# A block-triangular solve regrouped from two head pairs to four, and its rows emitted as a stream of their own

## Chip, cores and metric

One core of one Trainium2 chip runs the program in one launch. The metric is the device time of one execution in microseconds. Engines are named as the profile names them: PE (matmul), PEld (its weight loads), DVE (vector), ACT (scalar), POOL (GpSimd), SP (which here only issues DMAs); "ACTq" and "SPq" are DMA issues standing in an engine's instruction stream.

## What is computed

The network has a first block of two layers (retention, HGRN2, gated FFN) and a second block of two layers (sliding-window attention beside an RWKV7 recurrence, a conv FFN, a gated embedding). The sequence has 512 tokens, the model width is 1024. The change lies in the second block's mixer, in the recurrence, which has 16 heads of width 64:

```python
def step(state, inp):
    r_t, w_t, k_t, v_t, a_t, b_t = inp
    sa = jnp.einsum('bhvk,bhk->bhv', state, a_t)
    state = (state * w_t[:, :, None, :] + sa[..., None] * b_t[:, :, None, :]
             + v_t[..., None] * k_t[:, :, None, :])
    return state, jnp.einsum('bhvk,bhk->bhv', state, r_t)
```

The kernel does this in chunks of 64 tokens. A chunk needs the inverse of a unit lower triangular 64x64 matrix for each head; the kernel inverts its two 32x32 diagonal blocks by forward substitution on DVE and joins them by matmuls.

## The kernel before

Heads go in eight pairs, 0 to 7 (two heads of 64 on 128 partitions). For each of the second block's two layers `mixer2` does this:

- `rw_low` makes what all pairs share. Then the **attention stage**: the stream K (`keys`, which runs `rw_a` for a pair: projection, decays, and the triangular products into the tile `x2`, L1158) and the stream A (`attention`). `rw_a` of pairs 0 and 1 runs first alone, the rest beside attention.
- `rw_solve`, called by `keys` after each two pairs, sends the diagonal blocks through DRAM (`ls`) into `lu`, one block on a partition, so that 31 rows of the substitution work on all blocks at once. Each row is two DVE instructions, L1185 (`tm` = a column of `lu` times a row of `tt`) and L1186 (`tt` += `tm`), each needing the one before it. Two pairs have 2 pairs x 2 heads x 8 chunks x 2 blocks = 64 blocks; they stand twice on the 128 partitions, and each half of the partitions makes 16 of the 32 columns. The result goes to DRAM (`ts`, L1189). There are four such solves in a layer and eight in all.
- The **recurrence stage**: the stream `preps` (`rw_prep` of a pair: projections of r and v, loads of `wx`, `bk`, `x2` and of the solved blocks into `tb` at L1220, products) and the stream `seqs` (`rw_seq`: eight dependent steps, each a matmul L1317, a copy `sv` on DVE L1319 that the next step needs, and a copy on ACT L1320). A pair's prep waits for its solve and for the sequence two pairs back.

Projections are products of fp32 split into a high and a low part (L303, L304, L305); their weights are split by ACT (L287) and by POOL in the attention stage or DVE in the recurrence stage (L288). `interleave` merges the streams by a planned clock: a generator yields how long PE is busy and how long the stream then rests. `rw_solve` yields nothing, so in the plan a solve takes no time; `solved[b]` holds its planned end, 55 us after the call. The framework then moves instructions within each engine's stream by a model of its own, and each engine runs its stream in order. The tiles of the attention stage give their memory to those of the recurrence stage, so that `rdg` and `tb` are cleared (L1466, POOL) only when the last pair's `x2` has been read by its DMAs (L1174).

## Time and profile before

| what | value |
|---|---|
| time, median of 3 runs | 4030.81 us (4030.28 to 4038.12) |
| profiled execution, its own time | 4036.65 us |
| its span, first to last instruction | 4034.8 us |
| PE, DVE, ACT, POOL busy | 93%, 66%, 44%, 14% |
| mean granted clock of PE | 0.97 |

The span is what the profiler saw between the first and the last instruction of that execution; its own time is what was measured around it. A busy PE is not a PE at its peak, since matmuls overlap and their ends are modelled; the weight loads (PEld) follow the amount of matmul work more closely. In the first layer of the second block the attention stage runs from about 1495 to 1797 us and the recurrence from 1798 us to about 2110 us; the second layer repeats this 1300 us later.

### The profile page before, as it was taken

What the parts mean: (1) busy time and instruction counts of PE and PEld (TensorE: products, weight loads), DVE (VectorE), ACT (ScalarE), POOL (GpSimd) and SP (SyncE); (2) the same over time, 40 slices, a digit from 0 to 9 for tenths busy, and PEclk for the clock granted to TensorE, in tenths of its full rate; (3) what the DMA queues carried; (4) which work ended last, traced back from release to release, by engine and by line L of the source; (5) the groups of instructions that cost most, each with busy time, mean ns of one, the idle gap of its engine ahead of it and who ended that gap; (6) DMA issues with size and microseconds to landing.
All of it is one profiled execution on the core that took longest, in us unless ns stands there. A gap on an engine that the chain in (4) does not pass through costs nothing.

```text
span 4034.8 us, 56574 instructions
## 1 busy us (share of the span) xinstructions
PE 3762.3 (93%) x19888; PEld 3117.2 (77%) x19888; DVE 2667.9 (66%) x5595; ACT 1774.9 (44%) x3727; POOL 576.6 (14%) x515
## 2 busy tenths in 40 slices
PE   7998999999999988889999999998888989999998
PEld 6877888888888876657778888896665777888887
DVE  7888444555644567887664676687788775476667
ACT  4433333544433352435553554455344555354444
POOL 0201000110100033222110200014331220020001
PEclk9999999999999998989999999999888999999999
DMA  8466333312333343343227433344334323743334
GB/s 287 153 204 189 97 94 95 94 48 63 100 95 96 91 147 105 97 128 109 91 65 255 124 107 92 99 153 152 96 98 130 110 81 101 234 126 97 94 96 137
DMA packets 316573, 487.34 MB, mean 121 GB/s; under 512 B 79744, under 2 KB 127744, under 8 KB 316160
## 3 DMA queue, kind: packets, MB, share of 16 engines
q1 hardware_dynamic: 240256, 422.82, 34.0%
q10 hardware_dynamic: 76032, 60.90, 4.7%
q8 instruction: 157, 2.57, 0.3%
q14 instruction: 128, 1.05, 0.1%
HBM read 422.72 MB, written 60.88 MB: 120 GB/s over the span
## 4 chain that ended last, share of the span: by engine, by line
PE 55%; DVE 13%; ACT 3%; issue 3%; POOL 1%; DMA 1%; ACTq 0%; SPq 0%; POOLq 0%; DVEq 0%
PE ps L303 15%; PE ps L304 15%; PE ps L305 15%; DVE tm L1185 2%; PE ps L1317 1%; DVE tt L1186 1%; PE ps L1300 1%; PE ps L1157 1%; DVE ro L946 1%; DVE wl L288 1%; PE ps L983 1%; ACT wh L287 1%; PE ps L1023 1%; PE ps L1280 1%; PE ps L1285 1%
## 5 line engine op out<-in xcount | busy, mean ns | idle before, releaser
L303 PE MATMUL ps<-hi,wh 128*128 128x512 f32 (+1 forms) x4384 | 1635.3, 374 | 41.5 <-DVE ro L946 18.1
L305 PE MATMUL ps<-hi,wl 128*128 128x512 f32 (+1 forms) x4384 | 1622.1, 371 | 9.7 <-DVE wl L288 5.2
L304 PE MATMUL ps<-lo,wh 128*128 128x512 f32 (+1 forms) x4384 | 1622.7, 371 | 7.8 <-DVE lo L449 4.6
L287 ACT ACTIVATE wh<-raw 128x512 fp32r<-128x512 f32 (+1 forms) x1158 | 710.1, 620 | 1281.8 <-PE ps L304 1065.7
L288 DVE TENSOR_TENSOR wl<-raw,wh 128x512 fp32r<-128x512 f32 (+1 forms) x1005 | 690.8, 693 | 515.9 <-ACT wh L287 487.1
L303 PEld LDWEIGHTS ps<-hi,wh 128*128 128x128 f32 x4384 | 840.6, 192 | 181.3 <-issue 19.6
L305 PEld LDWEIGHTS ps<-hi,wl 128*128 128x128 f32 x4384 | 841.4, 192 | 143.7 <-DVE wl L288 7.8
L304 PEld LDWEIGHTS ps<-lo,wh 128*128 128x128 f32 x4384 | 842.5, 192 | 138.4 <-DVE lo L449 4.9
L288 POOL TENSOR_TENSOR wl<-raw,wh 128x512 fp32r<-128x512 f32 (+1 forms) x153 | 200.1, 1318 | 1193.2 <-ACT wh L287 1165.2
L1381 POOL TENSOR_TENSOR x<-x,ys 128x256 f32<-128x256 f32 x48 | 43.6, 909 | 862.9 <-DVE ys L1380 793.0
L482 DVE SCALAR_TENSOR_TENSOR ad<-ad,cact 128x1024 f32<-128x1024 f32 x96 | 116.7, 1220 | 29.2 <-DMA ad<-in_ada 29.1
L175 DVE TENSOR_TENSOR acc<-acc,sq 128x256 f32<-128x256 f32 (+1 forms) x175 | 96.1, 552 | 25.2 <-ACT sq L174 23.1
L1157 PE MATMUL ps<-bk,adg 128*128 128x192 f32 x256 | 67.2, 384 | 46.5 <-DVE bk L1147 20.5
L1319 DVE COPY sv<-ps 64x64 f32<-64x64 f32 x224 | 49.5, 221 | 90.4 <-PE ps L1317 87.6
L1185 DVE TENSOR_TENSOR tm<-lu,tt 128x126 f32<-128x126 f32 (+22 forms) x248 | 100.1, 404 | 9.0 <-DMA lu<-ls 4.0
L1580 DVE TENSOR_TENSOR u<-ps,r 128x512 f32<-128x512 f32 x88 | 60.5, 690 | 67.7 <-PE ps L305 67.0
L1317 PEld LDWEIGHTS ps<-sv,add 128*128 128x128 f32 (+1 forms) x512 | 77.9, 189 | 31.9 <-issue 8.8
L1292 POOL TENSOR_SCALAR add<-rdg 64x512 f32<-64x512 f32 x32 | 51.5, 1609 | 351.3 <-DVE add L1301 226.6
L1157 PEld LDWEIGHTS ps<-bk,adg 128*128 128x128 f32 x256 | 47.3, 216 | 64.8 <-issue 34.2
L1317 PE MATMUL ps<-sv,add 128*128 128x64 f32 (+1 forms) x512 | 91.1, 272 | 3.7 <-DVE sv L1319 2.3
L1320 ACT ACTIVATE y<-ps 64x64 f32<-64x64 f32 x256 | 54.7, 216 | 88.7 <-DVE sv L1319 49.5
L1186 DVE TENSOR_TENSOR tt<-tt,tm 128x126 f32<-128x126 f32 (+22 forms) x248 | 80.7, 325 | 3.7
(356 smaller groups left out, 5168.7 us busy)
## 6 DMA issues: line engine op xcount, KB each, us to landing
raw<-in_q_win SPq DMA_DIRECT2D x224, 256.0 KB, 2.9
ad<-in_ada SPq DMA_DIRECT2D x96, 512.0 KB, 4.4
raw<-in_q_w_up SPq DMA_DIRECT2D x184, 256.0 KB, 2.7
raw<-in_win SPq DMA_DIRECT2D x98, 256.0 KB, 3.1
raw<-in_w_val SPq DMA_DIRECT2D x92, 256.0 KB, 2.6
raw<-in_w_gate SPq DMA_DIRECT2D x92, 256.0 KB, 2.8
raw<-in_q_w_down SPq DMA_DIRECT2D x74, 256.0 KB, 2.6
raw<-in_w_down SPq DMA_DIRECT2D x64, 256.0 KB, 2.6
```

The source lines that it names most:

```text
L175: nc.vector.tensor_tensor(out=self.acc[:, cs], in0=self.acc[:, cs], in1=q, op=ADD)
L287: nc.scalar.activation(h, raw, AF.Copy)
L288: self.lo_eng.tensor_tensor(out=l, in0=raw, in1=h.bitcast(F32), op=SUB)
L303: nc.tensor.matmul(o, h, ah, start=k == first, stop=False)
L304: nc.tensor.matmul(o, h, al, start=False, stop=False)
L305: nc.tensor.matmul(o, l, ah, start=False, stop=k == last)
L482: nc.vector.scalar_tensor_tensor(out=raw, in0=raw, scalar=1.0, in1=self.cact, op0=MUL, op1=MUL, accum_out=m)
L1157: nc.tensor.matmul(o, ad[:, c], bk[:, c], start=True, stop=True)
L1185: nc.vector.tensor_tensor(out=t, in0=lc, in1=tt[:, 0:c, j:j + 1].to_broadcast([P, c, n]), op=MUL)
L1186: nc.vector.tensor_tensor(out=tt[:, 0:c, j + 1:32], in0=tt[:, 0:c, j + 1:32], in1=t, op=ADD)
L1317: nc.tensor.matmul(o, add[h][rows, c], c3(sv[h])[rows, c], start=True, stop=True)
L1580: nc.vector.tensor_tensor(out=u, in0=pj(ff), in1=r2, op=MUL)
```

## The change

One solve now takes four pairs, so 128 blocks, one on each partition, and every partition makes all 32 columns. Row j works on j + 1 columns instead of j // 2 + 1. There are two solves in a layer (`V` streams): the first for pairs 0 to 3 starts in the attention stage once pair 3's `x2` is there, the second for pairs 4 to 7 starts with the recurrence. Each row is emitted by itself and the stream then rests 3.5 us of planned time in the attention stage and 3.0 us in the recurrence. The blocks of each pair are sent to `ls` right after its `rw_a`, by the new `rw_lower`. The starting values `ttinit` become identity matrices; `lu`, `tt` and `tm` have one buffer each. `lu` is filled by one DMA and `ts` written by one, instead of two each.

```diff
--- before.py
+++ after.py
@@ -86,10 +86,7 @@
     hs[64:, 1] = 1.0
     c["hsel"] = hs
     c["blk1"] = np.kron(np.eye(2), np.ones((64, 64))).astype(np.float32)
-    tti = np.zeros((P, 16, 32), np.float32)
-    for cc in range(16):
-        tti[np.arange(P), cc, 2 * cc + np.arange(P) // 64] = 1.0
-    c["ttinit"] = tti
+    c["ttinit"] = np.tile(np.eye(32, dtype=np.float32), (P, 1, 1))
     c["rope2c"] = np.stack([invf[np.arange(P) % 32], np.where(q % 2 == 0, -1.0, 1.0)], axis=1).astype(np.float32)
     masks.append(mm == tt)
     c["lvmask"] = np.concatenate(masks, axis=1).astype(np.float32)
@@ -1162,33 +1159,34 @@
             nc.scalar.dma_start(st[n], src)
         yield 2.6, 1.0
 
-    def rw_solve(self, sts):
-
-
-        nc = self.nc
-        ls = self.dram("ls", (32, 2, 32, 32), 4)
-        for q, st in enumerate(sts):
-            for h in range(2):
-                for b in range(2):
-                    r, u = 64 * h + 32 * b, 16 * q + 8 * h
-                    nc.scalar.dma_start(ls[u:u + 8, b].rearrange("c t s -> t c s"), st["lm"][r:r + 32, :, 0, 32 * b:32 * b + 32])
+    def rw_lower(self, ls, i, x2):
+
+        for h in range(2):
+            for b in range(2):
+                r, u = 64 * h + 32 * b, 16 * i + 8 * h
+                self.nc.scalar.dma_start(ls[u:u + 8, b].rearrange("c t s -> t c s"), x2[r:r + 32, :, 0, 32 * b:32 * b + 32])
+
+    def rw_solve(self, sts, ls, gap):
+
+
+        nc = self.nc
         lu = self.rw.tile([P, 32, 32], F32, name=self.name("lu"), tag="lu", bufs=1)
-        tt = self.rw.tile([P, 16, 32], F32, name=self.name("tt"), tag="tt", bufs=2)
-        tm = self.rw.tile([P, 136], F32, name=self.name("tm"), tag="tm", bufs=2)
-        for m in range(2):
-            nc.sync.dma_start(lu[64 * m:64 * m + 64], ls.rearrange("u b t s -> (u b) t s"))
+        tt = self.rw.tile([P, 32, 32], F32, name=self.name("tt"), tag="tt", bufs=1)
+        tm = self.rw.tile([P, 256], F32, name=self.name("tm"), tag="tm", bufs=1)
+        nc.sync.dma_start(lu, ls.rearrange("u b t s -> (u b) t s"))
         nc.sync.dma_start(tt, self.I["ttinit"])
+        yield 0.0, 3.0
         for j in range(31):
-            n, c = 31 - j, j // 2 + 1
+            n, c = 31 - j, j + 1
             t = tm[:, 0:n * c].rearrange("p (c i) -> p c i", c=c)
             lc = lu[:, j + 1:32, j:j + 1].rearrange("p i o -> p o i").to_broadcast([P, c, n])
             nc.vector.tensor_tensor(out=t, in0=lc, in1=tt[:, 0:c, j:j + 1].to_broadcast([P, c, n]), op=MUL)
             nc.vector.tensor_tensor(out=tt[:, 0:c, j + 1:32], in0=tt[:, 0:c, j + 1:32], in1=t, op=ADD)
-        ts = self.dram("ts", (64, 16, 2, 32), 4)
-        for m in range(2):
-            nc.scalar.dma_start(ts[:, :, m], tt[64 * m:64 * m + 64])
+            yield 0.0, gap
+        ts = self.dram("ts", (128, 32, 32), 4)
+        nc.scalar.dma_start(ts, tt)
         for q, st in enumerate(sts):
-            st["ts"] = ts.rearrange("(u b) a m i -> u b (a m) i", b=2)[16 * q:16 * q + 16]
+            st["ts"] = ts.rearrange("(u b) a i -> u b a i", b=2)[16 * q:16 * q + 16]
 
     def mu_cols(self, l, j):
         i = self.idx[f"mu{l}"] + j
@@ -1433,14 +1431,21 @@
                         yield 5.2, 0.0
 
         st = [dict() for _ in range(8)]
-        solved = {-1: 0.0}
-
-        def keys(bs):
-            for b in bs:
-                for i in (2 * b, 2 * b + 1):
-                    yield from self.rw_a(l, i, H, st[i])
-                self.rw_solve(st[2 * b:2 * b + 2])
-                solved[b] = max(self.now + 4.0, solved[b - 1]) + 55.0
+        solved = {}
+        ls = [self.dram("ls", (64, 2, 32, 32), 4) for _ in range(2)]
+
+        def keys(pairs):
+            for i in pairs:
+                yield from self.rw_a(l, i, H, st[i])
+                self.rw_lower(ls[i // 4], i % 4, st[i]["lm"])
+                st[i]["lower"] = True
+
+        def solve(b, gap):
+            while "lower" not in st[4 * b + 3]:
+                yield 0.0, 0.5
+            yield 0.0, 2.0
+            yield from self.rw_solve(st[4 * b:4 * b + 4], ls[b], gap)
+            solved[b] = self.now + 3.0
 
         self.S = "G"
         for j in self.HEAD2[3:]:
@@ -1455,8 +1460,8 @@
             nc.gpsimd.memset(self.adg, 0.0)
             for t in self.bk:
                 nc.vector.tensor_copy(t[:, :, 2], self.id2.rearrange("p (o d) -> p o d", o=1).to_broadcast([P, 8, 64]))
-            self.interleave([("K", keys((0,)))])
-            self.interleave([("K", keys((1, 2, 3))), ("A", self.attention(l, H, od, pre[9]))])
+            self.interleave([("K", keys(range(2)))])
+            self.interleave([("V", solve(0, 3.5)), ("K", keys(range(2, 8))), ("A", self.attention(l, H, od, pre[9]))])
         with ExitStack() as es:
             self.rb = es.enter_context(self.tc.tile_pool(name="rb", bufs=1))
             self.rdg = [self.rb.tile([P, 8, P], F32, name=f"rdg{j}") for j in range(2)]
@@ -1468,7 +1473,7 @@
 
             def preps():
                 for i in range(8):
-                    while solved[i // 2] > self.now or i >= 2 and "seq" not in st[i - 2]:
+                    while solved.get(i // 4, 1e9) > self.now or i >= 2 and "seq" not in st[i - 2]:
                         yield 0.0, 0.5
                     yield from self.rw_prep(l, i, H, st[i])
 
@@ -1488,7 +1493,7 @@
                     nc.scalar.dma_start(md[m], g)
 
             self.lo_eng = nc.vector
-            self.interleave([("A", seqs()), ("K", preps())])
+            self.interleave([("V", solve(1, 3.0)), ("A", seqs()), ("K", preps())])
             self.S = "G"
             for _ in gates():
                 pass
```

In the rows of after, line numbers are two or three lower than those of the same code before: the solve's two lines are L1183 and L1184, the copy `sv` is L1317.

On DVE, in layer one, where the first solve of before begins (`lo` is the low half of small weights, `vt` an evacuation for attention, `t`, `ic`, `bk` belong to `rw_a` of pair 2). Before:

```order
L1065 TENSOR_SCALAR lw_13707<-lw_13707 128x512
L278 TENSOR_TENSOR lo_14150<-lora_14146,hi_14149 64x128
L1185 TENSOR_TENSOR tm_13397<-lu_13395,tt_13396 128x31
L1186 TENSOR_TENSOR tt_13396<-tt_13396,tm_13397 128x31
L1185 TENSOR_TENSOR tm_13397<-lu_13395,tt_13396 128x30
L1186 TENSOR_TENSOR tt_13396<-tt_13396,tm_13397 128x30
L1185 TENSOR_TENSOR tm_13397<-lu_13395,tt_13396 128x58
L1186 TENSOR_TENSOR tt_13396<-tt_13396,tm_13397 128x2x29
L1185 TENSOR_TENSOR tm_13397<-lu_13395,tt_13396 128x56
L1186 TENSOR_TENSOR tt_13396<-tt_13396,tm_13397 128x2x28
```

The same place after:

```order
L275 TENSOR_TENSOR lo_14084<-lora_14080,hi_14083 64x128
L965 COPY vt_13464<-ps_13614 128x512
L1138 TENSOR_SCALAR t_13876<-ic_13630,om_13058,om_13056 128x512
L1140 SCALAR_TENSOR_TENSOR ic_13630<-ic_13630,kk_13770 128x512
L1144 TENSOR_TENSOR bk_13141<-zs_13433,wi_13768 128x8x64
L1143 SCALAR_TENSOR_TENSOR bk_13141<-ic_13630,wi_13768 128x8x64
L940 TENSOR_TENSOR ro_13677<-ps_13640,cos_13454 128x512
```

The 62 solve instructions that began here are gone from this place, and `rw_a`'s and attention's own instructions (`ro` is attention's rotary step) follow each other. The first solve of after begins amid `rw_a` of pair 4, at about the place where the second solve of before stood; 231 places of the DVE stream lie between its first and its last instruction, with those of the other two streams between its rows.

On DVE, in the sequence of pair 0 (`sv` are the copies that the next step waits for). Before:

```order
L1319 COPY sv_15886<-ps_16161 64x64
L288 TENSOR_TENSOR wl_16332<-raw_16330,wh_16331 128x512
L1248 TENSOR_TENSOR zs_16047<-ps_16153,zs_16087 128x512
L1319 COPY sv_15887<-ps_16161 64x64
L1319 COPY sv_15886<-ps_16195 64x64
L288 TENSOR_TENSOR wl_16354<-raw_16352,wh_16353 128x512
L1319 COPY sv_15886<-ps_16247 64x64
L1319 COPY sv_15887<-ps_16195 64x64
L1319 COPY sv_15887<-ps_16247 64x64
```

The same place after:

```order
L1184 TENSOR_TENSOR tt_15569<-tt_15569,tm_15570 128x12x20
L1317 COPY sv_15677<-ps_15963 64x64
L1317 COPY sv_15676<-ps_15997 64x64
L1183 TENSOR_TENSOR tm_15570<-lu_15568,tt_15569 128x247
L1184 TENSOR_TENSOR tt_15569<-tt_15569,tm_15570 128x13x19
L1317 COPY sv_15676<-ps_16051 64x64
L1183 TENSOR_TENSOR tm_15570<-lu_15568,tt_15569 128x252
L1184 TENSOR_TENSOR tt_15569<-tt_15569,tm_15570 128x14x18
L1183 TENSOR_TENSOR tm_15570<-lu_15568,tt_15569 128x255
L1184 TENSOR_TENSOR tt_15569<-tt_15569,tm_15570 128x15x17
L1317 COPY sv_15677<-ps_15997 64x64
L1183 TENSOR_TENSOR tm_15570<-lu_15568,tt_15569 128x256
```

Rows of the second solve now stand between the copies; before, the last solve was over at this point. In the stream of after, the last row of this solve stands behind the `rdg` instructions of pair 3 and ahead of those of pair 4, whose prep is the first to need its result.

On ACT, at the end of the attention stage (`zs` evacuates pair 0's r projection for the recurrence, `wh` splits weights, the DMAs send pair 7's and pair 6's tiles). Before:

```order
L1162 DMA x_15690<-x_15665 128x1536
L1174 DMA ls_15692<-x_15382 32x8x32 x2
L1174 DMA ls_15692<-x_15665 32x8x32 x4
L1058 ACTIVATE zs_15822<-ps_15785,om_13054 128x512
L287 ACTIVATE wh_15827<-raw_15826 128x512
L287 ACTIVATE wh_15845<-raw_15844 128x512
L1424 ACTIVATE gt_18441<-ps_18442 128x512
```

After:

```order
L1159 DMA bk_15523<-bk_13142 1024x1x128
L1055 ACTIVATE zs_15610<-ps_15573,om_13054 128x512
L284 ACTIVATE wh_15810<-raw_15809 128x512
L284 ACTIVATE wh_15828<-raw_15827 128x512
L1055 ACTIVATE zs_15650<-ps_15613,om_13054 128x512
L284 ACTIVATE wh_18336<-raw_18335 128x512
L1159 DMA x_15525<-x_15496 128x1536
L1167 DMA ls_13076<-x_15496 32x8x32 x4
L284 ACTIVATE wh_15850<-raw_15849 128x512
```

The evacuations of pair 0 and the splits of pair 1's weights now stand ahead of the DMAs that wait for the last `x2`. On SP the loads of those weights likewise moved ahead of the load of `lu`.

## Rows read from the trace of the kernel before

**Rows 1.** The page: busy us, share of the span, instructions of each engine.

```profile
PE 3762.3 (93%) x19888; PEld 3117.2 (77%) x19888; DVE 2667.9 (66%) x5595; ACT 1774.9 (44%) x3727; POOL 576.6 (14%) x515
```

**Rows 2.** Stretches of both attention stages: length, busy of PE, PEld, DVE, ACT, POOL; PEclk, DMA, GB/s.

```profile
1560.00:1600.00 40.00, 27.41 (x101) 20.81 (x100) 36.68 (x86) 6.54 (x11) 14.89 (x13) 0.75 0.24 72
1600.00:1660.00 60.00, 55.42 (x274) 39.52 (x273) 49.18 (x123) 26.90 (x89) 20.24 (x17) 0.94 0.30 90
1680.00:1800.00 120.00, 101.99 (x463) 68.74 (x462) 101.62 (x304) 50.40 (x149) 23.54 (x20) 0.86 0.34 101
...
2860.00:2900.00 40.00, 27.40 (x101) 20.64 (x101) 33.99 (x82) 6.81 (x18) 14.24 (x12) 0.74 0.23 61
```

**Rows 3.** Chain that ended last, 1550:1605, 1670:1725, 1745:1800, 1800:1845, shares by line.

```profile
by line: DVE tm L1185 17.0%; issue 11.7%; PE ps L303 9.7%; PE ps L305 9.3%; DVE tt L1186 9.3%; DVE ro L946 8.8%; PE ps L304 8.6%; DMA lu<-ls 7.7%; DVE bk L1146 3.0%; POOL ro L947 2.4%; DVE ro L943 2.3%; POOL wl L288 2.3%; PE ps L983 1.5%; A
by line: issue 24.0%; DVE tm L1185 11.5%; DVE ro L946 10.1%; DVE tt L1186 8.8%; PE ps L1023 6.3%; PE ps L1157 5.6%; POOL adg L1150 5.3%; PE ps L1012 5.2%; PE ps L983 4.8%; PE ps L1121 3.8%; DVE x L1158 3.1%; PE ps L1133 2.9%; DVE lw L1065 2
by line: DVE tm L1185 12.0%; DVE tt L1186 11.9%; DMA lu<-ls 8.0%; PE ps L1157 7.2%; PE ps L1023 6.4%; DVE sc L988 5.0%; DVE x L1158 4.5%; DVE am L989 4.3%; PE ps L983 4.3%; issue 4.2%; ACTq L1174 4.2%; DVE sc L1001 3.8%; PE ps L1012 3.5%; D
by line: DVE tm L1185 19.8%; DVE tt L1186 16.4%; DVE rdg L1217 10.9%; DMA lu<-ls 9.8%; issue 8.9%; DVE zs L1228 7.1%; DVE wl L288 4.5%; DVE add L1301 3.4%; PE ps L304 2.8%; PE ps L303 2.8%; PE ps L305 2.8%; ACT rbb L1265 2.5%; DVE add L1243
```

**Rows 4.** The solve's two lines, 1545:1800 and then 1800:2100: busy us, mean ns.

```profile
L1185 DVE TENSOR_TENSOR tm<-lu,tt 128x126 f32<-128x126 f32 (+22 forms) x93 | 40.1, 431 | 2.9 <-DMA lu<-ls 2.0
L1186 DVE TENSOR_TENSOR tt<-tt,tm 128x126 f32<-128x126 f32 (+22 forms) x93 | 30.5, 328 | 1.1
...
L1185 DVE TENSOR_TENSOR tm<-lu,tt 128x126 f32<-128x126 f32 (+22 forms) x31 | 10.4, 335 | 2.3 <-DMA lu<-ls 1.6
L1186 DVE TENSOR_TENSOR tt<-tt,tm 128x126 f32<-128x126 f32 (+22 forms) x31 | 9.4, 302 | 0.7
```

**Rows 5.** Timeline of single solve instructions and one POOL instruction: start, us, what.

```profile
1556.16 0.21 DVE L1185 TENSOR_TENSOR tm<-lu,tt 128x31 f32<-128x31 f32 x1 [1.98 <-DMA lu<-ls]
1556.40 0.19 DVE L1186 TENSOR_TENSOR tt<-tt,tm 128x31 f32<-128x31 f32 x1
...
1557.47 1.28 POOL L288 TENSOR_TENSOR wl<-raw,wh 128x512 fp32r<-128x512 f32 x1 [3.77 <-ACT wh L287]
1557.64 1.18 DVE L1185 TENSOR_TENSOR tm<-lu,tt 128x56 f32<-128x56 f32 x1
...
1571.91 0.30 DVE L1186 TENSOR_TENSOR tt<-tt,tm 128x133 f32<-128x133 f32 x1
...
1581.49 0.39 DVE L1185 TENSOR_TENSOR tm<-lu,tt 128x130 f32<-128x130 f32 x1
```

**Rows 6.** Timeline where attention ends and recurrence begins, PE, ACT, POOL, SP.

```profile
1794.81 0.39 PE L305 MATMUL ps<-hi,wl 128*128 128x512 f32 x1
1798.49 0.79 PE L303 MATMUL ps<-hi,wh 128*128 128x512 f32 x1 [3.29 <-ACT wh L287]
1797.23 0.69 ACT L1058 ACTIVATE zs<-ps,om 128x512 f32<-128x512 f32 x1 [12.29 <-DMA ls<-x]
1798.65 2.38 POOL L1466 MEMSET rdg<- 128x1024 f32 x2 [13.69 <-DMA ls<-x]
1798.58 1.09 SPq L1179 DMA_DIRECT2D lu<-ls  x2
```

**Rows 7.** Start of the recurrence, columns as in rows 2.

```profile
1798.00:1848.00 50.00, 42.36 (x218) 33.24 (x218) 44.80 (x100) 18.93 (x40) 17.01 (x13) 0.90 0.55 177
1848.00:1908.00 60.00, 55.00 (x358) 43.84 (x359) 41.18 (x92) 34.38 (x94) 11.80 (x10) 1.00 0.36 106
```

**Rows 8.** Pair 3's rdg, pair 4's block loads, the stores of solved blocks, their landing.

```profile
L1217 DVE TENSOR_TENSOR rdg<-zs,wx x2: 673/681/689, 1900.1 to 1901.4; 64x512 f32<-64x512 f32 x2
1934.59 1.86 SPq L1220 DMA_DIRECT2D tb<-ts  x4
L1189 ACTq DMA_DIRECT2D ts<-tt x16: 515/658/1317, 1599.5 to 3143.2; - x16
DMA to landing us min/median/max: 2.6/3.5/4.6
```

## Prediction

> **What bounds the kernel now.** I read the page first: PE is busy 93% of the span and DVE 66% [rows 1]. As a mean that says PE. So I went to the stage of the change and cut it into stretches. In 1560 to 1600, where the first solve runs, DVE is busy 36.7 of 40 us, PE 27.4, and its weight loads, which follow the amount of matmul work, 20.8 (0.52 of the stretch) at a granted clock of 0.75. In the next 60 us, with no solve, the weight loads make 39.5 of 60 (0.66). In 1680 to 1800, where two more solves run, they make 68.7 of 120 (0.57). Layer two repeats the first stretch, 27.4 us of PE in 40 [rows 2]. Then the chain of waits: the solve's two lines have 17.0% + 9.3% of 1550 to 1605, 20.3% of 1670 to 1725, 23.9% of 1745 to 1800 and 36.2% of 1800 to 1845 [rows 3]. In these stretches DVE decides, and a good part of the path is the solve. Its DVE time in a layer is 70.6 us for the three solves of the attention stage and 19.8 for the one at the start of the recurrence, 90.4 together [rows 4].
>
> **What a solve costs after.** Undisturbed, L1185 takes 0.21 us for 31 elements and 0.39 for 130, so 0.154 + 0.00182 n; L1186 takes 0.19 for 31 and 0.30 for 133, so 0.157 + 0.00108 n [rows 5]. The sum of (31 - j)(j // 2 + 1) over the 31 rows is 2856, of (31 - j)(j + 1) it is 5456. A solve of before is therefore 62 instructions with 9.6 us of fixed cost and 0.0029 x 2856 = 8.3 of elements, 17.9 us; one of after 9.6 + 15.8 = 25.4. Elements stay about the same in a layer (4 x 2856 against 2 x 5456); what is saved is fixed cost. Measured, the three in the attention stage take 23.5 each, 5.6 above 17.9, and the one in the recurrence 19.8, 1.9 above. The excess comes from POOL: an L1185 of 56 elements took 1.18 us, beginning just after POOL had begun an instruction of 1.28 us and ending with it, where the formula gives 0.26 [rows 5]. I take 5 us of excess in the attention stage and 3.5 in the recurrence: 30.5 and 29 us. DVE then gives back 90.4 - 59.5 = 31 us a layer, 40 in the attention stage, and the recurrence gets 9 more. What of this reaches the path, per layer:
>
> *A. The first solve leaves 1560 to 1600.* Upper bound: its lines' and the `lu` load's share of the path, (17.0 + 9.3 + 7.7)% of 55 = 18.7 us. Lower bound: the same weight loads at the rate of the next 60 us, 20.8 / 0.659 = 31.6 instead of 40, 8.4 us. Next late there are attention's rotary steps on DVE (8.8% + 2.3%) and the splits on POOL. I take 12.
>
> *B. Two solves of 47 us become one of 30.5 in 1670 to 1797.* Without any solve the weight loads of 1680 to 1800 at 0.659 would need 104.4 us, 15.6 less; the path's share of both is 20.3% and 23.9% of 55, 24.3 us. 35% of the work stays, so 16.5 of 47: 35% of 15.6 is 5.5, of 24.3 it is 8.5. Its rows stand between other streams' instructions, and whoever stands behind one waits at most about 1.0 us. I take 6; bounds 0 and 8.5.
>
> *C. Where the stages meet.* PE stops for 3.3 us, until ACT has split weights; ACT stood 12.3 us in front of pair 0's evacuation, in a stream that first had to issue `ls` DMAs of the last `x2` [rows 6]. After the change that evacuation and four splits come first, and PE has the matmuls of pair 1's projections ready. POOL's clearing of `rdg` still waits for the last `ls` DMA (13.7 us now) [rows 6]. I take 4 with the slow clock that follows the pause (a first matmul of 0.79 us against 0.39); bounds 0 and 6.
>
> *D. The recurrence's first 110 us.* DVE is busy 44.8 of the first 50 us and 41.2 of the next 60 [rows 7]. In the first 50 the 19.8 us go and about 8 come (the 11 rows that stand ahead of the first `sv` copy have 1606 elements: 22 x 0.155 + 4.7). DVE falls to 33 there, and weight loads at the rate of the next 60 (43.8 / 60) would need 45.5 us instead of 50: up to 4.5 gained. In the next 60 the other 21 us come: 62 of 60. DVE is then full, and the copies `sv`, on which the sequence hangs, stand behind rows of up to 0.62 us: for two pairs 28 copies, half of them behind one of 0.5, is 7 us if nothing covers it. Together +2.5; bounds -4.5 and +10.
>
> The rest costs nothing on the path as far as rows show. `lu`, `tt` and `ts` are moved by 6 issues in a layer instead of 20 (an issue of `ts` takes 0.66 us on ACT [rows 8]), of about the same bytes; `ls` keeps its 32, now after each pair. They go from ACT and SP, which are not what PE and DVE wait for in A and B; if that cover fails, 14 issues are under 10 us, already inside the bounds. The single buffer of `tt` makes the second start value wait for the first solve's store, which is issued ahead of the stage's end.
>
> **Sum.** Per layer -12 - 6 - 4 + 2.5 = -19.5, for two layers -39. Against the profiled execution's own 4036.65 us this is 3997.7. That execution is 5.8 us above the median of 4030.8, so the median should come to **3992 us**, 1% less.
>
> **The rivals.**
> *More than that.* If DVE alone decided wherever the path names it, all upper ends come true: -18.7 - 8.5 - 6 - 4.5 = -37.7 a layer, 3955. For it: the path's shares. Against: PE's and POOL's own queues stand right behind DVE. Chance 0.17.
>
> *POOL's collisions grow.* In 1680 to 1800 POOL runs 20 instructions, in the recurrence's first 110 us 23 [rows 2, 7]. A solve drawn out over some 80 us (from its place in the order) and 110 us meets 13 and 23 of them instead of those in a short stretch; at 0.9 us each (1.18 against 0.26) a solve costs 25.4 + 12 = 37 and 25.4 + 21 = 46. Then B is 2 and D +10: -8 a layer, 4015. Against: now 33 POOL instructions in the first and third stretch of rows 2 go with 17 us of excess, half a microsecond each, in solves that leave DVE hardly any other work. Chance 0.13. The Trainium skill speaks for this rival ("SBUF — State Buffer", section "SBUF: two separate sides"): a DVE instruction with two SBUF inputs and a GpSimd instruction that reads SBUF exclude each other, and the second waits for the whole of the first. The 1.18 us against 1.28 agree with that.
>
> *The wait only moves.* PE gets the lower end of A, and elsewhere its own queue and the weight splits take DVE's place: -8.4 + 0 + 0 + 2.5, about -6 a layer, 4019. For it: even in the solve-free 60 us the weight loads make only 66%. Chance 0.12.
>
> *Slower.* Pairs 4 to 7 now wait for the second solve; before, only 6 and 7 waited for the last. Its last row stands behind pair 3's `rdg`, which ran at 1901 us, and pair 4's blocks were loaded at 1934.6. Store and landing take 0.7 + 3.5 us [rows 8], and the load's issue 1.9: 27 us to spare. If DVE, at 62 of 60 us, lets the last row slip beyond that, every further microsecond holds up SP, the loads behind it and PE. A to C give 22, so it is slower from a slip of about 50 us a layer on; at 54 it is 4041. The numbers above show a slip of a few. Chance 0.06.
>
> *It doesn't do what it says.* The rows could have been put together again by the framework; the order shows them spread, in both stages. Chance 0.02.
>
> **The numbers.** Forecast 0.50 (3972 to 4010); the rest as above. The range of 3962 to 4022 leaves out the slower cases and half of the largest gain. A measurement of this kernel can tell about 0.2%, 8 us, from no change. Faster by more than that: forecast, the larger gain, and nearly all of the two small gains, 0.86. Slower 0.07, the same 0.07.
>
> **What would show it.** Right: 1560 to 1600 with PE above 33 of 40 us and a clock above 0.9; the solve's lines at 120 to 130 us in all for 248 instructions, a first and last row of 0.2 us and middle rows near 0.62 and 0.43; the attention stage about 20 us shorter in each layer; no pause of PE over 1 us where the stages meet; the recurrence as long as now, within 5 us. Wrong: solve instructions above 1 us more often than now, which is POOL; PE waiting at L1317 for `sv` by more than 10 us a layer; or pair 4's load of `tb` late on SP with `raw` loads behind it.

## The result and the profile after

The changed kernel takes 3974.43 us (median of 4 runs, 3970.11 to 3990.43) against 4033.84 for the kernel before beside it. The ratio is 0.986, 95% interval 0.9829 to 0.989. It is faster by 59 us where 39 was forecast, inside the range given, at the fast end of 3972 to 4010. The profiled execution ran 3977.14 us with a span of 3975.3; before it was 4034.8. Its line numbers are 2 or 3 lower than those of before (but L1466 is L1471).

The page of the changed kernel, the row that answers to [rows 1]:

```profile
PE 3748.1 (94%) x19888; PEld 3109.2 (78%) x19888; DVE 2617.1 (66%) x5347; ACT 1776.9 (45%) x3727; POOL 580.3 (15%) x515
```

Span less busy PE is 227 us; before it was 4034.8 - 3762.3 = 272. PE pauses 45 us less. The rest of the gain is not in the pauses.

Stretches of the changed kernel, which answer to [rows 2] (the last one is layer two, shifted by its lead of some 32 us) and to [rows 7]; columns as there:

```profile
1560.00:1600.00 40.00, 35.56 (x176) 27.47 (x174) 26.25 (x55) 14.27 (x36) 21.02 (x18) 1.00 0.28 92
1600.00:1660.00 60.00, 55.46 (x263) 38.13 (x261) 45.20 (x106) 24.87 (x79) 17.31 (x14) 0.94 0.31 98
1660.00:1780.00 120.00, 110.17 (x566) 78.85 (x566) 106.02 (x286) 58.61 (x170) 26.96 (x22) 0.99 0.35 113
2828.00:2868.00 40.00, 35.55 (x173) 27.14 (x172) 27.91 (x57) 13.07 (x35) 20.84 (x18) 1.00 0.28 86
...
1780.00:1830.00 50.00, 43.04 (x271) 34.03 (x270) 45.13 (x86) 25.02 (x63) 19.81 (x15) 1.00 0.57 185
1830.00:1890.00 60.00, 53.70 (x319) 43.43 (x318) 54.25 (x122) 27.21 (x71) 15.50 (x12) 0.93 0.33 100
```

Where the first solve stood, PE runs 176 matmuls in 40 us instead of 101, at a granted clock of 1.00 (2.4 GHz) instead of 0.75, a mean of the 2.4 and 1.2 GHz levels. In 1660 to 1780 DVE is as full as ever, 106 of 120 us, and yet PE is at 110 of 120. DVE's busy share therefore did not decide there. At the start of the recurrence DVE is busy as long as before in the first 50 us and longer in the next 60; PE runs 271 matmuls instead of 218 and then 319 instead of 358, so about as many in all.

The solve's two lines in the attention stage, then in the recurrence of layer one, which answer to [rows 4]:

```profile
L1183 DVE TENSOR_TENSOR tm<-lu,tt 128x31 f32<-128x31 f32 (+15 forms) x31 | 15.8, 510 | 0.4
L1184 DVE TENSOR_TENSOR tt<-tt,tm 128x31 f32<-128x31 f32 (+15 forms) x31 | 12.2, 393 | 0.4
...
L1183 DVE TENSOR_TENSOR tm<-lu,tt 128x31 f32<-128x31 f32 (+15 forms) x31 | 17.1, 550 | 0.4
L1184 DVE TENSOR_TENSOR tt<-tt,tm 128x31 f32<-128x31 f32 (+15 forms) x31 | 14.9, 482 | 0.6
```

28.0 and 32.0 us, forecast 30.5 and 29; 119.9 us for all 248 instructions. The start of the second solve in the recurrence, single instructions of DVE and two of POOL beside them (start, us):

```profile
1784.62 0.20 DVE L1183 TENSOR_TENSOR tm<-lu,tt 128x31 f32<-128x31 f32 x1
1784.86 0.19 DVE L1184 TENSOR_TENSOR tt<-tt,tm 128x31 f32<-128x31 f32 x1
...
1787.68 0.99 DVE L1183 TENSOR_TENSOR tm<-lu,tt 128x87 f32<-128x87 f32 x1
1788.70 1.43 DVE L1184 TENSOR_TENSOR tt<-tt,tm 128x87 f32<-128x87 f32 x1
...
1787.02 1.98 POOL L1290 TENSOR_SCALAR add<-rdg 64x512 f32<-64x512 f32 x1 [0.77 <-DVE rdg L1215]
1788.97 1.05 POOL L1221 TENSOR_TENSOR bh<-bk,wx 128x512 f32<-128x512 f32 x1
...
1793.08 0.43 DVE L1241 TENSOR_TENSOR add<-ps,c_maski 64x256 f32<-64x256 f32 x1
```

The rows do stand apart: behind the third row come instructions of other streams, among them the products `add`, on which PE hangs. In all, the trace has 185 other DVE instructions among the 62 of the first solve, which last from 1663.3 to 1759.3 us, and 127 among those of the second, 1784.6 to 1884.8. The solves of before weren't solid blocks either, but denser: 62 instructions in 42 to 51 us, with 29 to 69 others among them.

Where the stages meet, in the timeline (compare [rows 6]):

```profile
1778.25 0.63 ACT L284 ACTIVATE wh<-raw 128x512 fp32r<-128x512 f32 x1 [5.58 <-DMA ls<-x]
...
1780.26 1.84 POOL L1471 MEMSET rdg<- 128x1024 f32 x2 [14.39 <-DMA ls<-x]
```

PE's pause of 3.29 us is gone: it has pair 1's projections to do. POOL still waits 14.4 us for `ls`, and in its place PE then waits 1.6 us for `rdg` and 3.4 for `add`. The chain that ended last breaks off in the trace of the changed kernel, so [rows 3] have no answer; PE's waits in the recurrence take their place. Changed kernel, 1776 to 2090 (who waits, for whom: us, times, longest), then the kernel before, 1797 to 2124:

```profile
PE ps L1244 <- DVE add L1241: 7.2, 5, 3.4
PE ps L1337 <- DVE y L1331: 4.6, 3, 3.9
PE ps L1298 <- DVE add L1299: 3.0, 6, 1.9
```

```profile
PE ps L1246 <- DVE add L1243: 17.7, 7, 4.3
...
PE ps L1317 <- DVE sv L1319: 1.2, 1, 1.2
...
PE ps L1339 <- DVE y L1333: 0.4, 1, 0.4
```

The wait for `add` falls by 10.5 us, that for `y` rises by 4.2. The wait for `sv`, which I had priced at 7, was 1.2 us and is 0.8.

How far the changed kernel is ahead, from the first and last starts that the trace gives for a line (us against before, less than zero is earlier):

| point | layer one | layer two |
|---|---|---|
| first `x2` product | +1.5 | -30.5 |
| first value product of attention | -15.0 | -45.7 |
| last `x2` product | -20.1 | -51.0 |
| first product of a prep (L1234) | -20.4 | -50.1 |
| first step of a sequence (L1315) | -31.9 | -61.7 |
| end of the sequences | -34.6 | -61.8 |

These points don't enclose the same work. In layer one the changed kernel has 19 matmuls fewer than before from the first `x2` to the first value product, 43 more from there to the last `x2`, 22 more from there to the first prep, 54 fewer from there to the end of the sequences (43 of them ahead of the first step) and 9 more behind; in all both have 19888. So the lengths alone don't tell what a stretch gained. The table of stretches below takes the matmuls' own time off.

### The profile page after: what moved, and what is told of

It is laid out like the page before. It is cut to its first block, busy times and chain, and to the rows that moved or that the text cites. A ratio compares the mean times of both kernels' runs of the same rounds, so it can differ in the third digit from the quotient of the medians.

```text
span 3975.3 us, 56298 instructions
## 1 busy us (share of the span) xinstructions
PE 3748.1 (94%) x19888; PEld 3109.2 (78%) x19888; DVE 2617.1 (66%) x5347; ACT 1776.9 (45%) x3727; POOL 580.3 (15%) x515
## 5 line engine op out<-in xcount | busy, mean ns | idle before, releaser
L479 DVE SCALAR_TENSOR_TENSOR ad<-ad,cact 128x1024 f32<-128x1024 f32 x96 | 117.3, 1227 | 23.9 <-DMA ad<-in_ada 23.6
L1315 PEld LDWEIGHTS ps<-sv,add 128*128 128x128 f32 (+1 forms) x512 | 77.0, 190 | 33.9 <-ACT y L1318 15.6
L1290 POOL TENSOR_SCALAR add<-rdg 64x512 f32<-64x512 f32 x32 | 54.3, 1698 | 301.9 <-PE ps L1315 226.5
L1317 DVE COPY sv<-ps 64x64 f32<-64x64 f32 x224 | 49.5, 221 | 72.9 <-PE ps L1315 69.3
L1315 PE MATMUL ps<-sv,add 128*128 128x64 f32 (+1 forms) x512 | 91.7, 274 | 3.6 <-DVE sv L1317 1.6
L784 ACT ACTIVATE cv<-u,vec 128x512 f32<-128x512 f32 x88 | 71.4, 814 | 26.1 <-DVE u L1585 26.1
L993 ACT ACTIVATE sc<-sc,am 128x256 f32<-128x256 f32 (+1 forms) x128 | 60.1, 471 | 47.0 <-DVE am L989 46.1
L1154 PEld LDWEIGHTS ps<-bk,adg 128*128 128x128 f32 x256 | 45.1, 205 | 44.9 <-issue 19.0
```

What stands on the lines that cost most here:

```text
L479: nc.vector.scalar_tensor_tensor(out=raw, in0=raw, scalar=1.0, in1=self.cact, op0=MUL, op1=MUL, accum_out=m)
L784: nc.scalar.activation(t, p, AF.Identity, bias=b, scale=w[2])
L993: nc.scalar.activation(view(hd), view(hd), AF.Exp, bias=nm[:, hd:hd + 1], accum_out=sm[:, hd:hd + 1])
L1154: nc.tensor.matmul(o, ad[:, c], bk[:, c], start=True, stop=True)
L1315: nc.tensor.matmul(o, add[h][rows, c], c3(sv[h])[rows, c], start=True, stop=True)
```

## Experiments

**Theory 1**: the time comes from the 124 DVE instructions a layer that grouping saves. **Theory 2**: it comes from the place, rows thinly spread between other streams' instructions instead of close together before what PE waits for. **Theory 3**: it comes from the new order of `ls` stores and evacuations. "The changed kernel" ran once more among them. All are compared as ratios to the kernel before on the same chip. Three columns are from one profiled execution: PE's pauses (span less busy PE), the mean granted clock, and the loss to the clock, which I worked out over the whole span from stretches of 10 us as PE's busy time times (1 - granted clock).

| kernel | ratio (95%) | PE's pauses | clock | loss to it |
|---|---|---|---|---|
| before | 1 | 272 | 0.970 | 88 |
| changed | 0.986 (0.9829 to 0.989) | 227 | 0.979 | 60 |
| changed, again | 0.9857 (0.9835 to 0.988) | 224 | 0.979 | 61 |
| regrouped, both in one go | 1.0042 (1.0028 to 1.0056) | 261 | 0.960 | 131 |
| old solve, spread | 1.000 (0.999 to 1.001) | 254 | 0.968 | 99 |
| second in one go | 0.9903 (0.989 to 0.9917) | 245 | 0.976 | 69 |
| stores per pair alone | 1.0018 (1.0009 to 1.0027) | 258 | 0.968 | 99 |
| changed, no rows | 0.9898 (0.9882 to 0.9915) | 228 | 0.971 | 89 |
| before, no rows | 0.9838 (0.9823 to 0.9853) | 228 | 0.976 | 72 |
| stores one step later | 0.9879 (0.9864 to 0.9893) | 236 | 0.973 | 80 |
| contiguous operand | 0.9848 (0.9833 to 0.9863) | 225 | 0.977 | 64 |
| old solve, new places | 0.9956 (0.9944 to 0.9968) | 248 | 0.971 | 89 |
| tight gaps | 0.9883 (0.9866 to 0.990) | 232 | 0.976 | 75 |
| wide gaps | 0.9916 (0.9898 to 0.9934) | 240 | 0.977 | 67 |

The next table gives the excess of four stretches, in layer one and two: their length less the time that their matmuls need, each priced at the median distance between starts of its form in the changed kernel (0.227 us for 512 columns, which most of the moved ones have). That price is an estimate. A goes from the first `x2` to the first value product, B from there to the last `x2`, C from there to the first prep, D from there to the end of the sequences. Outside them the excess is 201 to 219 us in all kernels (206 before, 210 changed).

| kernel | A | B | C | D |
|---|---|---|---|---|
| before | 25.5, 25.7 | 32.7, 33.0 | 7.0, 6.6 | 56.9, 56.9 |
| changed | 13.2, 14.8 | 18.0, 18.1 | 1.8, 2.6 | 54.9, 57.4 |
| changed, again | 13.5, 13.1 | 19.0, 18.0 | 2.2, 1.7 | 60.5, 54.9 |
| regrouped, both in one go | 13.3, 14.9 | 43.2, 47.0 | 0.5, 0.0 | 72.8, 70.2 |
| old solve, spread | 20.1, 23.4 | 26.1, 18.8 | 9.4, 7.9 | 67.0, 69.6 |
| second in one go | 15.3, 13.2 | 19.2, 18.1 | 2.3, 3.5 | 63.8, 63.4 |
| stores per pair alone | 22.3, 25.6 | 34.2, 37.2 | 3.7, 3.9 | 62.4, 62.1 |
| changed, no rows | 13.5, 14.5 | 29.3, 28.3 | 0.7, 0.0 | 53.3, 53.5 |
| before, no rows | 16.7, 21.2 | 16.9, 13.0 | 1.5, 1.4 | 53.6, 54.9 |
| old solve, new places | 20.1, 23.5 | 26.2, 19.6 | 8.5, 8.6 | 58.0, 58.1 |
| tight gaps | 13.4, 15.1 | 23.6, 26.6 | 1.9, 1.9 | 59.3, 59.8 |
| wide gaps | 13.3, 16.3 | 18.7, 23.0 | 2.8, 2.8 | 61.1, 59.9 |

### Grouping without spreading

```diff
-            yield 0.0, gap
+            if gap:
+                yield 0.0, gap
...
-            solved[b] = self.now + 3.0
+            solved[b] = self.now + (3.0 if gap else 33.0)
...
-            self.interleave([("V", solve(0, 3.5)), ...
+            self.interleave([("V", solve(0, 0)), ...
-            self.interleave([("V", solve(1, 3.0)), ...
+            self.interleave([("V", solve(1, 0)), ...
```

> The new solve (four pairs, 62 instructions) with both its instances traced in one go again, 31 rows in a block, and everything else as in the changed kernel. Theory 1 (the time comes from DVE instructions saved by regrouping, wherever they stand): the solve's lines stay near 120 us and the kernel stays at 3974 to 3988. Theory 2 (the time comes from rows standing between other streams instead of in a block before PE's suppliers): the lines stay near 120 us but the kernel goes back to 4008 to 4025, with PE's longest pauses behind the blocks, above all before the first sequence of the recurrence.

4054.88 us against 4038.38: slower than the kernel before, beyond even what theory 2 said, with 123.7 us of solve lines. So fewer instructions alone don't make the kernel faster. Emitted in one go doesn't mean a solid block: in the trace at least one instruction of another stream stands between any two of the first solve, 73 in all, and it lasts from 1666.1 to 1726.6 us, where the changed kernel's takes 96 us. So this run tests how close the rows stand. What that does shows in 10 us stretches while the first solve runs (columns as in rows 2):

```profile
1660.00:1670.00 10.00, 10.00 (x58) 8.15 (x56) 8.02 (x24) 5.11 (x18) 1.79 (x2) 1.00 0.22 76
1670.00:1680.00 10.00, 8.02 (x39) 5.67 (x40) 9.78 (x31) 4.21 (x12) 2.89 (x3) 0.83 0.17 52
1680.00:1690.00 10.00, 7.57 (x33) 4.33 (x29) 9.99 (x23) 4.05 (x16) 5.17 (x4) 0.80 0.34 105
1690.00:1700.00 10.00, 8.93 (x33) 7.33 (x33) 9.78 (x21) 0.63 (x1) 1.92 (x2) 0.69 0.30 93
...
1710.00:1720.00 10.00, 7.79 (x28) 4.67 (x27) 9.84 (x19) 3.81 (x10) 4.71 (x4) 0.50 0.31 105
1720.00:1730.00 10.00, 8.07 (x35) 5.67 (x35) 8.90 (x24) 2.44 (x7) 3.29 (x3) 0.50 0.25 85
```

and the same place in the changed kernel:

```profile
1670.00:1680.00 10.00, 8.84 (x49) 5.71 (x48) 9.81 (x32) 5.34 (x18) 2.13 (x4) 1.00 0.32 108
1680.00:1690.00 10.00, 5.98 (x22) 4.67 (x21) 9.83 (x23) 2.08 (x6) 4.74 (x4) 0.83 0.44 127
1690.00:1700.00 10.00, 8.18 (x47) 5.07 (x46) 9.74 (x22) 6.12 (x18) 1.44 (x1) 1.00 0.23 81
1700.00:1710.00 10.00, 9.61 (x50) 6.23 (x51) 9.62 (x24) 4.96 (x14) 3.80 (x4) 1.00 0.13 46
1710.00:1720.00 10.00, 9.90 (x58) 7.87 (x57) 9.85 (x31) 5.15 (x18) 2.56 (x2) 1.00 0.49 161
```

DVE is full in both, but among the dense rows the solve has 32.6 of DVE's 58.4 busy us, in the changed kernel 28.0 of 91.6. With dense rows PE pauses 1 to 2.4 us in every 10 from 1670 on; its clock falls, in the end to 0.50 (1.2 GHz) for 20 us, in which it gets 63 matmuls done. In the changed kernel PE has one larger gap, 4 of 10 us, with a mean clock of 0.83, and is back at 1.00 at once.

The total hides two effects. In A, which the first solve has left, this kernel gains as much as the changed one; it loses that again, and more, in B (43 and 47 us of excess against 18) and D.

### Spreading without grouping

```diff
+    self.interleave([("V", solve((0, 1, 2), 1.75)), ("K", keys(range(2, 8))), ("A", ...
+    self.interleave([("V", solve((3,), 3.0)), ("A", seqs()), ("K", preps())])
```

> The old solve (two pairs, 62 instructions, four of them in a layer), but as a stream of its own with a gap between rows: three in the attention stage, the fourth in the recurrence. Theory 1 (DVE instructions saved): the solve's lines stay at 155 to 180 us for 496 instructions and the kernel at 4012 to 4030. Theory 2 (place): the kernel reaches 3975 to 3992, though DVE is busy 35 to 60 us longer than in the changed kernel.

4037.41 against 4038.38, no difference. The attention stage got 9.2 us shorter in layer one, but the third solve's rows ran on to 1816.6, 36 us past the last `x2` product, close together, and from there to the end of the sequences 7.7 us were lost. So this kernel has dense rows again, in a new place, and its first solve still begins at 1556 us. It does not test theory 2 cleanly.

### The second solve in one go

The same edit as in the first experiment, for the second solve only.

> The changed kernel with the second solve of each layer, at the start of the recurrence, traced in one go; the first one keeps its gaps. Theory 2 says that the 11 us a layer that the trace of the changed kernel shows between the first preparation and the first sequence come from the block's absence: 3992 to 4002, and the stretch from the first preparation to the first sequence long again, 36 to 44 us instead of 26. Theory 1: 3972 to 3980, since the same instructions run. Rival to both (theory 3, the order where the stages meet: ls stores and pair 0's evacuation): also 3972 to 3980.

3997.38 us. In the time theory 2 is right to the number; its stretch is not as long as it said. In the trace the second solve takes 57.7 us instead of 100. First and last starts of the preps' first products and of the sequences' steps, kernel before, changed, this one:

```profile
L1236 PE MATMUL ps<-rdg,bk x128: 271/275/377, 1808.1 to 2056.1; 128*128 128x128 f32 x128
L1317 PE MATMUL ps<-sv,add x256: 217/275/324, 1845.8 to 2112.7; 128*128 128x64 f32 x112, 64*128 64x64 f32 x16
```

```profile
L1234 PE MATMUL ps<-rdg,bk x128: 270/275/377, 1787.7 to 2025.0; 128*128 128x128 f32 x128
L1315 PE MATMUL ps<-sv,add x256: 217/275/324, 1813.9 to 2078.2; 128*128 128x64 f32 x112, 64*128 64x64 f32 x16
```

```profile
L1235 PE MATMUL ps<-rdg,bk x128: 270/275/422, 1798.1 to 2045.7; 128*128 128x128 f32 x128
L1316 PE MATMUL ps<-sv,add x256: 217/275/474, 1831.0 to 2101.1; 128*128 128x64 f32 x112, 64*128 64x64 f32 x16
```

From the first prep to the first sequence it is 37.7, 26.2 and 32.9 us; from there to the last sequence's start 266.9, 264.3 and 270.1. Of the 11.5 us by which the change shortened the way from the first prep to the first sequence, some 8.8 are matmuls that now stand elsewhere (43 of 179), so the expectation had too much to explain. Over all of D the excess is 63.8 and 63.4 us, 6 to 9 more than in the changed kernel's first profile, 3 to 9 more than in its second. And PE waits for `add` as long as it did before (1786 to 2113 us):

```profile
PE ps L1245 <- DVE add L1242: 17.6, 7, 3.6
```

Without the rows (below) this wait is 8.1 us, in the changed kernel 7.2. So the long wait belongs to a dense second solve. Regrouping with both in one go is 57.5 us slower than this kernel: that is the first solve's dense rows, most of it loss to the clock (131 against 69).

### The stores per pair alone

```diff
+                    self.rw_lower(ls[b], i % 2, st[i]["lm"])
```

> The kernel before with one part of the change alone: the ls stores of a pair are issued behind that pair's x2 instead of ahead of the solve. Theory 3 (order on ACT where the stages meet, forecast term C): 4020 to 4026, with the pause of PE of 3.3 us at the boundary gone or under 1.5 us. Theories 1 and 2: 4030 to 4037, no difference that can be told, because the solves stand where they stood.

(The same four stores leave `rw_solve`.) 4046.57 against 4038.38: slower by 0.18%, no theory's number, and theory 3 has the wrong sign. At the boundary it was half right: PE's pause of 3.3 us is 0.2, but one of 2.7 us for `tb` follows, and the excess of C falls by 3 us while B and D grow. The pauses of PE fall by 14 us in all, but its busy time rises by 26, at no higher clock; why is open.

### Without the substitution's rows

The two instructions of each row are left out of the changed kernel and of the kernel before.

> The changed kernel without the 31 rows of the substitution (both instructions of each row left out, so the inverse that it stores is the identity); the plan, the gaps and all DMAs stay. Its distance from the changed kernel's 3974 is what the rows still cost there. If rows that stand between other instructions hide in DVE's idle time, 3960 to 3972. If DVE's time counts wherever it stands (60 us a layer), 3920 to 3945.

> The kernel before without the 31 rows of the substitution (both instructions of each row left out; the plan and all DMAs stay). Before, the rows are 90 us of DVE a layer in blocks of 20 to 24. If a block costs the path about what it takes on DVE, 60 to 80 us a layer: 3880 to 3915. If only the amounts of the forecast's upper ends (33 us a layer without the boundary) can be had: 3960 to 3975. Theory 1 says that it comes out below the changed kernel without rows or like it; theory 2 that it comes out like it, since nothing else of the change would then matter.

3998.39 and 3974.33 us, beside 4040.02. Taking all rows out of the kernel before gives 0.9838, the changed kernel with all its rows 0.986: within their intervals the change brings what having no substitution at all would bring there. By stretches the two sums are not alike: A gains more by the change, B by leaving the rows out. And leaving the rows out of the changed kernel makes it no faster: PE's pauses stay at 228 us. The rows are hidden but for 1 to 7 us a layer in D. That it gets slower, by 15 us (by the ratios) to 24, goes with the clock (a loss of 89 against 60), as in these stretches of the changed kernel without rows:

```profile
1730.00:1740.00 10.00, 8.22 (x40) 5.16 (x40) 9.86 (x23) 6.12 (x18) 4.12 (x3) 0.95 0.22 78
1740.00:1750.00 10.00, 8.98 (x27) 5.43 (x26) 6.47 (x23) 3.50 (x13) 0.00 (x0) 0.50 0.17 55
1750.00:1760.00 10.00, 10.00 (x36) 6.87 (x35) 4.28 (x14) 5.36 (x16) 0.00 (x0) 0.53 0.37 118
1760.00:1770.00 10.00, 10.00 (x57) 7.97 (x56) 1.84 (x3) 3.42 (x8) 0.00 (x0) 1.00 0.16 54
```

PE pauses under 2 of 10 us, its clock falls to 1.2 GHz, and it is busy 19 of 20 us for 63 matmuls; the next 10 us, at 1.00, hold 57. The bounds that took DVE's time for the path's (3880 to 3915 and 3920 to 3945) are wrong here.

### The stores one step later

```diff
-                self.rw_lower(ls[i // 4], i % 4, st[i]["lm"])
...
+                    if n == 0 and late is not None:
+                        self.rw_lower(ls[late // 4], late % 4, st[late]["lm"])
```

> The changed kernel, with the ls stores of a pair (but for pairs 1, 3 and 7) issued on ACT one step later, behind the evacuations of the next pair's first projections instead of right behind the pair's own x2. The stores placed per pair alone made the kernel before 8 us slower, in the attention stage. Theory 3a (ACT stands at the issue until x2 is there, and what is queued behind comes late): 3962 to 3970. Rival (the 8 us belong to something else, such as the solve's start moving on DVE): 3972 to 3978.

3989.76 us, ratio 0.9879. Neither the gain of theory 3a nor the rival's 3972 to 3978. Its attention stages are as long as the changed kernel's (251.2 and 254.7 us from first to last `x2` product, against 254.0 and 255.7); from the first step of a sequence to the end of the sequences it is 8.7 and 5.9 us longer, and the loss to the clock there grows by some 9.5 and 6.5.

### A contiguous operand

```diff
-            lc = lu[:, j + 1:32, j:j + 1].rearrange("p i o -> p o i").to_broadcast([P, c, n])
+            lc = lu[:, j:j + 1, j + 1:32].to_broadcast([P, c, n])
```

> The changed kernel with the first instruction of each row reading a row of lu (elements side by side) instead of a column (one element every 128 bytes); so it computes with the wrong triangle of the factor. If the stride makes the first instruction cost 1.82 ns an element against 1.08 of the second, the first line goes from 66 to about 50 us in all, 4 us less in a solve; of the time, if a quarter to a half of DVE's saving reaches the path, 3966 to 3971. If the slope has another cause (a broadcast operand), the line stays at 66 and the kernel at 3974.

3978.55 us, 0.9848. Two forms of the row's first instruction, here and then in the changed kernel (busy us, mean ns):

```profile
L1183 DVE TENSOR_TENSOR tm<-lu,tt 128x231 f32<-128x231 f32 x8 | 3.1, 388 | 0.0
L1183 DVE TENSOR_TENSOR tm<-lu,tt 128x31 f32<-128x31 f32 x8 | 1.6, 200 | 0.4 <-DMA lu<-ls 0.4
```

```profile
L1183 DVE TENSOR_TENSOR tm<-lu,tt 128x231 f32<-128x231 f32 x8 | 4.4, 549 | 0.0
L1183 DVE TENSOR_TENSOR tm<-lu,tt 128x31 f32<-128x31 f32 x8 | 1.7, 209 | 0.1
```

The line falls from 65.8 to 51.1 us in all: (388 - 200) / 200 = 0.94 ns an element instead of 1.70. The stride was the cost. The Trainium skill says so ("SBUF — State Buffer", section "Door 1: The DMA port swizzle"): accesses that cross to a new line of 16 bytes each pay a penalty, and here every element lies 128 bytes on; these rows agree. The time does not move: 15 us of DVE less are worth nothing where the rows are already hidden.

### The old solve in the new places

```diff
-    solve((0, 1, 2), 1.75) ... solve((3,), 3.0)
+    solve((0, 1), 1.75) ... solve((2, 3), 1.5)
```

(against the spread kernel above)

> The old solve (two pairs, 62 instructions, four of them in a layer) as a stream, with the places of the changed kernel: the first two in the attention stage, the other two in the recurrence. Against the changed kernel it has 124 instructions of DVE more in a layer, about 0.155 us each by their fixed part, 19 us; the place is the same. Theory 2 (place alone): 3970 to 3985. Theory 1 in the form that is left (place and fewer instructions both needed, since one alone brought nothing): 3995 to 4020.

4017.28 against 4035.23. Its two lines, 160.9 us in all:

```profile
L1186 DVE TENSOR_TENSOR tm<-lu,tt 128x126 f32<-128x126 f32 (+22 forms) x248 | 88.1, 355 | 21.9 <-DMA lu<-ls 12.6 <-issue 4.2
L1187 DVE TENSOR_TENSOR tt<-tt,tm 128x126 f32<-128x126 f32 (+22 forms) x248 | 72.8, 294 | 5.7
```

Spreading and this assignment of solves to stages bring 18 us, the changed kernel 40 more. But the places are not those of the changed kernel, as the expectation says: the first solve of a layer still runs here from 1556 to 1628 us, where the changed kernel has none, and the third from 1769 to 1824 with up to 19 of its instructions in a row. In the excess some 16 of the 40 us lie in A, where that first solve stands, 10 in B, 13 in C and 4 in D (the stretches outside give 3 back). So most of it lies in stretches in which solves stand at other times, or closer, than in the changed kernel; what the smaller count of instructions is worth was not isolated. Nor was the old solve of pairs 0 and 1 tried at a later start.

### The changed kernel again, and two other gaps

> The changed kernel once more, beside the three others of this call. Any theory: a ratio of 0.983 to 0.989 to the kernel before. If the slow-clock stretches belong to the kernel's own order and not to chance, the profile has them at the same places as the first one (a granted clock near 1.00 in the last 100 us of the attention stage, PE idle near 25.6 us in the stage).

> The changed kernel with gaps of 2.75 and 2.25 instead of 3.5 and 3.0 between a solve's rows. Same instructions, slightly other places. If rows between other instructions are hidden and a few us of placement do not matter, 3970 to 3980. Rival (the time hangs on where PE pauses and its clock falls, which any shift of order changes): PE's idle time within 5 us a layer of the changed kernel's, the time up to 20 us away, and the distance in the time at a low granted clock.

> The changed kernel with gaps of 4.25 and 3.75. Theories as for the tight gaps: 3970 to 3980, or up to 20 us away with the distance in the time at a low granted clock. The first solve then ends about 23 us later, still inside the attention stage, the second as much later, near pair 4's load at 1907: if that load comes late, PE waits there and the recurrence grows by 5 us or more a layer.

3972.83, 3987.90 and 3998.93 us. With tight gaps pauses are 8 us more and the loss to the clock 14; with wide gaps 16 and 6. So a change of under a microsecond in the plan's gaps moves the time by 26 us for the wide ones; the 15 of the tight ones are at the edge of the noise (their interval overlaps that of the changed kernel). The rows themselves hardly moved: the first solve runs from 1664.1 to 1760.1 us with tight gaps, from 1660.5 to 1758.1 with wide ones, and its end did not come 23 us later. So these runs test small shifts in the order around the rows, not their density. The rival is right on the size; that pauses stay within 5 us a layer holds for the tight gaps and not for the wide ones, whose attention stages pause 3 us more each and whose recurrences 3 and 4. Pair 4's load with wide gaps came at 1910.18, 3 us later than in the changed kernel, and PE did not wait for it. The clock's pattern of the changed kernel returned in the attention stage of layer two (a loss of 6.9 against 7.8), in its recurrence it was 5.4 against 8.3, in layer one's recurrence 12.4 against 5.4: partly the kernel's, partly chance.

The nine executions of the changed kernel go from 3964.17 us at a mean clock of 0.981 to 3994.31 at 0.973. Over 110 executions of all kernels, each against the mean of its own kernel, 0.001 of clock goes with 2.8 us (regression of time on clock) to 3.9 (the other way round). The mean clock is 0.9687 in 39 executions of the kernel before and 0.9779 in these nine: 26 to 36 of the 61 us between their means go with the clock. The kernel without rows (0.9710) is 21.6 us above the changed one, of which 19 to 27 go with it: by this estimate they are equal at equal clock. It is a correlation; no run held the clock and changed something else.

## Why the prediction was right in sign and short in size

*A, the first solve leaves*: forecast -12. The length changes by -16.5 and -15.2, but some 4 us of that are matmuls that now stand later; the excess falls by 12.3 and 10.9. In its place PE got 35.6 of 40 us (over 33 forecast) at a clock of 1.00 (over 0.9). Right in mechanism and size: in every kernel whose first solve begins at 1657 us or later, or whose rows are left out there, the excess of A is 13 to 16 us, wherever one begins near 1556 it is 20 to 26, and in the kernel before without rows 17 and 21.

*B, two solves become one*: forecast -6, bounds 0 and 8.5. The length changes by -5.1 and -5.3 with 43 matmuls more in it; the excess falls by 14.7 and 14.9. **This is the term that was mis-sized.** It reckoned that no solve at all would bring 15.6 us, and that "35% of the work stays", so that only 35% of this could be had. What stays costs almost nothing once its rows stand thinly: the excess is 18 us with them, 17 and 13 in the kernel before without any row, and 43 and 47 with the same rows close together. That so much came of it is in part luck. PE's pauses in B fell by 6.5 us and the loss to the clock by 13, and that loss comes back in kernels whose rows stand no closer (excess 24 and 27 with tight gaps) or are left out (29 and 28).

*C, where the stages meet*: forecast -4. The first prep's product comes 0.3 earlier and 0.9 later relative to the last `x2`, but PE does 22 matmuls more ahead of it, so the excess falls by 5.2 and 4.0. The pause of 3.29 us is gone, as said. Right in size; wrong that no pause over 1 us would be left, since pauses of 1.6 and 3.4 us follow.

*D, the recurrence's first 110 us*: forecast +2.5, bounds -4.5 and +10. From the first prep to the end of the sequences the length changes by -14.2 and -11.7, but 54 matmuls, some 12 us, moved out of it; the excess (of the whole recurrence, since my points don't cut it at 110 us) changes by -2.0 and +0.5, which is nothing that can be told (it is 60.5 and 54.9 in the second profile). Right in size, wrong in its reasons. DVE is busy 45.1 of the first 50 us where 33 was forecast, and 54.3 of the next 60 where 62 was. It priced PE's wait for `sv` at 7 us, and that is 0.8; what changed is the wait for `add`, and a dense second solve brings it back and takes back 17 us of the 59.

By the excess the four are -34.2 and -29.3 instead of -19.5 a layer; outside these stretches 4 us come back in all. Of the 10 to 15 us a layer that the sum fell short, B is 9. Of the time gained, about half goes with the granted clock: the loss to it falls from 88 to 60 us, of which B has 26; pauses fall from 272 to 227. The forecast had the clock only inside A's rates and in C's slow first matmul.

*Solve's cost*: 119.9 us, forecast 120 to 130. Right.

*The rivals.* "More than that" (3955) named DVE as what decides; its number was nearer to the outcome than its reason, since without rows the time is no better. "POOL's collisions grow": 28.0 and 32.0 us of rows, where the clean formula gives 25.4, are 2.6 and 6.6 us above it, forecast 5 and 3.5, and the rival's 37 and 46 us did not come. Single rows such as the 0.99 and 1.43 us above take 0.7 and 1.2 us more than the formula gives, beside two POOL instructions that read SBUF; seven instructions above 1 us in a layer, where before there were 15, are too few to matter. That such pairs exclude each other is what the Trainium skill states ("SBUF — State Buffer", section "SBUF: two separate sides"), and these rows agree in kind; their ends differ from POOL's by 0.1 to 0.3 us. "The wait only moves": no; pauses fell by 45 us. "Slower": pair 4's load of `tb` came at 1907.17 us, the solve's last instruction at 1884.58, 22.6 us before, of which store and landing need 3.5. "It doesn't do what it says": the rows stand apart.

## What to carry to other kernels

In these runs small dependent instructions that stood close together on DVE held up the other streams' instructions there: PE made short pauses, and its clock fell. The same rows over 96 us instead of 60 left 25 to 29 us less of excess in a layer's attention stage. Grouping with dense rows, spreading the old solve, and spreading it over both stages brought +17, 0 and -18 us; grouping and thin rows together brought -59, as much as leaving the work out. The gain in A is simpler: the grouped solve has to start later, and so leaves a stretch in which the old one stood in the way.

When work is hidden, further cuts in it (15 us of DVE) are worth nothing, and what an edit then moves is where PE pauses, so compare granted clock and pauses before you give an edit its reason. And count the work between two points before you take the time between them for a gain: here 54 matmuls had moved out of the recurrence, and its length alone would have shown a gain of 12 us that is not there.

## What had not been expected of the hardware

Removing 120 us of DVE instructions made the kernel slower, 3998 against 3974 us, with the same pauses of PE (228 and 227 us) and a granted clock of 0.971 instead of 0.979. One fall of the clock to 0.50 over some 20 us came behind pauses of under 2 us in 10; a gap of 4 us in 10 elsewhere (a mean of 0.83 in those 10) was followed by 1.00 at once. Which pauses bring the clock down is left open by these runs.
